# Embedding products between the row pairs, a last down group by token halves, residual joins divided

## The chip, the cores and the metric

One Trainium2 chip; the kernel runs on one core. The metric is the device time of one execution in microseconds. The profiled execution is one such run, recorded by the hardware profiler.

## What is computed

One layer of a hybrid decoder on 1024 tokens of width 1024, in float32. What matters here is its second half:

```
h = h + mixed @ w_o                                   # mixed: attention and convolution, normed
a = rms_norm(h, ln_ffn_g) @ w_up                      # 1024 -> 2 x 2816
gate, up = split(a); gate = causal_dwconv(gate) + b
h = h + (silu(gate) * up) @ w_down                    # 2816 -> 1024
h = h + sigmoid(rms_norm(h, ln_ple_g) @ w_pg) * (p @ w_pe)   # p: 256 wide
```

`p @ w_pe` (the embedding product) depends on the inputs alone. A norm's factor 1/rms belongs to a token, so a product's result can be multiplied by it afterwards.

## The kernel before

The engines: TensorE (PE) multiplies, VectorE (DVE), ScalarE (ACT) and GpSimd (POOL) do the rest, SyncE (SP) issues the transfers. Features lie on the 128 partitions, in 8 rows `m`; tokens lie along the free axis, in two halves `hf` of 512. Each float32 operand is split into a rounded high part and a remainder (`hi`, `lo`), and each product is three matmuls 128x512: hi x hi, hi x lo, lo x hi (`mm3`, L101 to L103). PSUM has 8 banks of 128x512, which the tiles take in turn; a matmul group into a bank waits until what lay there before has been read.

*Rows.* `mixed @ w_o` is made for half 1 first, 8 rows `bh`, and then for half 0 in four pairs of rows, `A0` to `A3`: rows k and k + 4, tiles `bp`, 24 matmuls a pair. What follows a row (`row_rest`, L887 to L904): VectorE multiplies by a factor and adds the residual (`hm`, also stored to memory as `hD`), ScalarE makes `y` = `hm` x gain and squares `hm`, into PSUM, and VectorE adds the squares up (`fssq`).

*Products by Strassen.* `@ w_up` is done as 7 products for each of 22 chunks of features, on 2x2 blocks of activations and weights (a Winograd form). The four differences t1 to t4 of a pair's blocks (`forms_of`, L906 to L922, GpSimd and VectorE) and their high and low parts (`keep_form`, L873, tiles `forms`) are made once. Products are called (f, i), chunk and number; each is 12 matmuls, into `ux`, `uy` or `uz`. Weight blocks and GpSimd's sums of them (`wsum`, L984) are split into `wbh` and `wbl` some products ahead. `uv` is ScalarE's copy of product 1 (L1058), which frees its PSUM tile for product 2.

The list `order` sets the sequence of pairs and products, and `behind(n, d, rank, fn)` puts what follows a product d places later. The instructions of each engine stand in the order of the program there; in the down groups a scheduler orders them.

*Down.* `@ w_down` sums over the 22 chunks in 6 groups (`GROUPS`: 3, 4, 4, 4, 4, 3 chunks). In each group and for each row m, weights are loaded and split (L140, L143), and both halves are multiplied (12 matmuls each for 4 chunks, 9 for 3) and added to `h` (L1154). `acth`, `actl` are the parts of a chunk's activations. In group 4 GpSimd multiplies `h` by the norm's factor `rfb` (L1160) and adds the residual `hD` (L1163). In group 5 VectorE multiplies the product by `rfb` (`t`, L1157) and adds it (L1158).

*End.* Then come 2 rows of embedding products `b`, the gated inputs `fh`, `fl` of all 8 rows over 1024 tokens (ScalarE L1198, VectorE L1199; squares L1206, summed on GpSimd L1207), and 8 rows of `@ w_pg`, with one further row of embedding products after each. The norm's factor is made behind the first half row: token sums on TensorE (L156), a VectorE step (L158), a power on GpSimd (L160), then spread over the partitions by small matmuls (L165). `finish_` is the rest of an output row.

## Time and profile before

| | us |
|---|---|
| median of 3 runs | 1489.42 (1489.16 to 1489.54) |
| profiled execution | 1490.71 |
| its span in the profile | 1488.9 |
| TensorE busy in the span | 1433.8 (96%) |
| VectorE, ScalarE, GpSimd busy | 990.5, 584.2, 492.6 |

The matmuls are pipelined: a record lasts about 0.4 us, but where nothing waits the next starts 0.23 us later. TensorE's idle time is therefore the measure, and its granted clock. In the page's 40 slices TensorE falls below nine tenths at the very start and in three later places; two concern us, the row pairs (632 to 720 us) and the end of the down groups (about 1325 to 1375 us).

### The profile page before, as it was taken

The page shows a single profiled execution, that of the slowest core. Times are in us where ns is not written, and L with a number is a line of the kernel's source. Part 1 is how long each engine was busy: PE and PEld are TensorE (multiplying, and loading weights), DVE is VectorE, ACT ScalarE, POOL GpSimd, SP SyncE. Part 2 cuts the span into 40 slices and gives each one's busy share as a digit, 9 for nine tenths or more (in the row PEclk, how much of TensorE's full clock was granted, in tenths as well). Part 3 has the DMA queues.
Part 4 walks back from the last instruction along what each step waited for, and adds up shares of the span by engine and source line. Part 5 has one row for each costly group of instructions (what it writes and reads, how often), then busy time and mean ns, then how long its engine had stood idle before and what let it go on. Part 6 is the DMA issues. An engine that isn't in the chain of part 4 may idle for free.

```text
span 1488.9 us, 19441 instructions
## 1 busy us (share of the span) xinstructions
PE 1433.8 (96%) x7207; PEld 1168.9 (79%) x7207; DVE 990.5 (67%) x1588; ACT 584.2 (39%) x1190; POOL 492.6 (33%) x467
## 2 busy tenths in 40 slices
PE   7999999998999999986999999999999999997998
PEld 6787898996777777765888888888888888876887
DVE  7645566546778888777777777877774344469533
ACT  4110131237868889653323333233335112125211
POOL 3221242465445558245223333333310000474000
PEclk9999999999989999997999999999999999999999
DMA  6221214300000002241222222222235123341211
GB/s 250 82 71 56 75 58 155 104 1 1 1 1 1 1 1 86 93 149 63 72 74 68 71 85 85 86 86 85 78 114 184 57 106 114 103 160 69 71 43 43
DMA packets 48190, 115.50 MB, mean 78 GB/s; under 512 B 5472, under 2 KB 8160, under 8 KB 48096
## 3 DMA queue, kind: packets, MB, share of 16 engines
q1 hardware_dynamic: 48096, 114.26, 22.8%
q8 instruction: 57, 0.93, 0.3%
q14 instruction: 37, 0.30, 0.1%
HBM read 90.12 MB, written 24.12 MB: 77 GB/s over the span
## 4 chain that ended last, share of the span: by engine, by line
PE 55%; DVE 6%; ACT 2%; issue 2%; DMA 1%; POOL 1%; SPq 0%; ACTq 0%; DVEq 0%; POOLq 0%
PE uy L1018 12%; PE uz L1018 8%; PE ux L1018 8%; PE ba L102 6%; PE ba L103 6%; PE ba L101 6%; PE bv L753 2%; PE ba L719 1%; DVE forms L881 1%; ACT P L683 1%; DVE h L1158 1%; PE b L666 1%; DVE t L1157 1%; PE b L101 1%; PE b L667 0%
## 5 line engine op out<-in xcount | busy, mean ns | idle before, releaser
L1018 PE MATMUL uy<-forms,wbh 128*128 128x512 f32 x528 | 166.6, 397 | 0.0
L694 POOL TENSOR_SCALAR P<-P,sc,consts 128x64 f32<-128x64 f32 (+8 forms) x192 | 129.2, 683 | 103.6 <-DVE sc L692 98.0
L984 POOL TENSOR_TENSOR wsum<-wup,wup 128x512 f32<-128x512 f32 x44 | 71.8, 1632 | 234.5 <-DMA wup<-in_w_up 201.6
L102 PE MATMUL ba<-actl,wh 128*128 128x512 f32 x352 | 138.1, 394 | 1.7 <-DVE actl L1140 1.6
L103 PE MATMUL ba<-acth,wl 128*128 128x512 f32 x352 | 137.5, 393 | 0.0
L101 PE MATMUL ba<-acth,wh 128*128 128x512 f32 x352 | 137.2, 393 | 0.0
L998 DVE TENSOR_TENSOR wbl<-wsum,wbh 128x512 fp32r<-128x512 f32 x88 | 79.8, 907 | 66.3 <-ACT wbh L997 66.3
L1018 PE MATMUL uz<-forms,wbh 128*128 128x512 f32 x352 | 112.8, 401 | 8.3 <-DVE forms L881 3.3
L1018 PE MATMUL ux<-forms,wbh 128*128 128x512 f32 x352 | 111.9, 399 | 9.2 <-ACT uv L1058 9.2
L677 DVE TENSOR_REDUCE nmax<-b 128x1 f32<-128x64 f32 (+8 forms) x192 | 96.7, 539 | 36.0 <-PE b L669 35.3
L1018 PEld LDWEIGHTS uy<-forms,wbh 128*128 128x128 f32 x528 | 100.3, 190 | 23.4
L683 ACT ACTIVATE P<-b,nmax 128x64 f32<-128x64 f32 (+8 forms) x192 | 108.9, 576 | 19.8 <-DVE sc L692 12.1
L143 DVE TENSOR_TENSOR wl<-wraw,wh 128x1024 fp32r<-128x1024 f32 (+3 forms) x93 | 92.2, 995 | 31.7 <-ACT wh L140 14.4
L1018 PE MATMUL uy<-forms,wbl 128*128 128x512 f32 x264 | 104.7, 396 | 0.0
L1154 DVE TENSOR_TENSOR h<-h,ba 128x512 f32<-128x512 f32 x64 | 43.8, 686 | 89.9 <-PE ba L103 89.8
L719 PE MATMUL ba<-consts,P 128*128 128x128 f32 x592 | 91.2, 278 | 5.3 <-DVE pl L735 2.5
L142 POOL TENSOR_SCALAR wh<-wraw 128x1024 fp32r<-128x1024 f32 (+2 forms) x37 | 47.9, 1298 | 133.3 <-PE b L102 46.1
L140 ACT CAST wh<-wraw 128x512 fp32r<-128x512 f32 (+2 forms) x56 | 35.3, 647 | 143.5 <-PE ba L102 119.6
L1160 POOL TENSOR_TENSOR h<-h,rfb 128x1024 f32<-128x1024 f32 x8 | 22.4, 2795 | 205.9 <-DVE h L1154 203.5
L719 PEld LDWEIGHTS ba<-consts,P 128*128 128x128 f32 x592 | 68.9, 143 | 23.9 <-issue 7.7
L1018 PEld LDWEIGHTS ux<-forms,wbh 128*128 128x128 f32 x352 | 67.1, 191 | 25.4 <-ACT uv L1058 9.6
L1018 PEld LDWEIGHTS uz<-forms,wbh 128*128 128x128 f32 x352 | 67.4, 192 | 24.8 <-DVE forms L881 3.6
(306 smaller groups left out, 3854.3 us busy)
## 6 DMA issues: line engine op xcount, KB each, us to landing
wup<-in_w_up SPq DMA_DIRECT2D x88, 256.0 KB, 4.1
aD<-ua SPq DMA_DIRECT2D x22, 512.0 KB, 2.9
t<-aD SPq DMA_DIRECT2D x22, 512.0 KB, 4.5
wraw<-in_w_down SPq DMA_DIRECT2D x32, 256.0 KB, 5.6
wraw<-in_wA SPq DMA_DIRECT2D x13, 512.0 KB, 3.6
hinc<-in_xT SPq DMA_DIRECT2D x16, 256.0 KB, 3.4
h<-t SPq DMA_DIRECT2D x16, 256.0 KB, 2.4
hin<-h SPq DMA_DIRECT2D x16, 256.0 KB, 4.2
```

The lines of the kernel that those rows point to most:

```text
L101: pe.matmul(ps, ah, bh, start=first, stop=False)
L102: pe.matmul(ps, ah, bl, start=False, stop=False)
L103: pe.matmul(ps, al, bh, start=False, stop=last)
L142: pool.tensor_scalar(hi, raw, 1.0, 1.0, op0=OP.mult, op1=OP.mult)
L143: dve.tensor_sub(lo, raw, f32(hi))
L677: dve.tensor_reduce(nmax[:, b:b + 1], ps[:, o:o + w], axis=AX.X, op=OP.max, negate=True)
L683: act.activation(pr[:, pc:pc + w], ps[:, o:o + w], AF.Exp, bias=nmax[:, b:b + 1], accum_out=den[:, b:b + 1])
L694: pool.tensor_scalar(pr[:, pc:pc + w], pr[:, pc:pc + w], sc[:, b:b + 1], gates[:, t, hd * 3 + b:hd * 3 + b + 1], op0=OP.mult, op1=OP.mult)
L719: pe.transpose(pt[0:k, r * P:(r + 1) * P], probs[u, r][:, pc:pc + k], ident)
L984: pool.tensor_tensor(t, a, b, op=op)
L998: dve.tensor_sub(lo, y, f32(hi))
L1018: pe.matmul(ps, a[:, k], b, start=new and k == n_mm == 0, stop=k == 3 and n_mm == 2, skip_group_check=not new)
```

## The change

1. The 96 matmuls of the embedding products go from the end to a place between the row pairs: the list now runs A0, E0, E1, E2, A1, E3, E4, E5, A2, E6, E7, (0,1), A3, (1,1), (0,2), (1,2). ScalarE copies each result to SBUF, it is stored to memory (`eD`) and loaded again in `finish_` (`ein`). Their weights and `p` are loaded and split beside the `bh` rows (from `mid` on).
2. What follows a pair is written anew (`pair_rest`, `pair_end`): all four differences on VectorE, squares to SBUF, the sums of squares last, and the parts of t2, t3, t4 beside the next pair.
3. The groups are 3, 4, 4, 4, 3, 4. The last takes all 8 rows for token half 0 and then all for half 1, with its weights kept in 8 buffers (`wd`), and the gated input of a row and half is made at once from the PSUM tile `bd`. The norm's sums and spread go by halves.
4. The residual joins: `irb` = 1/`rfb` is made before group 0 (8 spread matmuls); GpSimd multiplies `hD` by it and adds it to `h`, rows 0 to 3 in group 1 and rows 4 to 7 in group 2. All of `h` is then multiplied by `rfb` in the last group.

```
-GROUPS = (3, 4, 4, 4, 4, 3)
+GROUPS = (3, 4, 4, 4, 3, 4)
...
-        if m == 0:
-            act.square(fs, hm)
-        else:
-            act.square(ps, hm)
-            dve.tensor_add(fs, ps, fs)
...
+    def row_square(m, hf, hm):
+        sq = fssq[:, hf * 512:(hf + 1) * 512] if m == 0 else S([P, 512], F32, "t2", 4)
+        act.square(sq, hm)
+        return sq
+
+    def row_norm(m, hf, sq):
+        if m:
+            fs = fssq[:, hf * 512:(hf + 1) * 512]
+            dve.tensor_add(fs, fs, sq)
+
+    def sub(nm, k, a, b):
+        z = yf[nm, k] = S([P, 512], F32, f"yt1{k}" if nm == "t1" else "yt", 1 if nm == "t1" else 4)
+        dve.tensor_sub(z, a, b)
+
+    def form_hi(nm, k, y):
+        both = S([P, 2, 512], F32R, f"form{nm}{k}")
+        form[nm][k] = both[:, 0], both[:, 1]
+        act.copy(form[nm][k][0], y)
+
+    def form_lo(nm, k, y):
+        hi, lo = form[nm][k]
+        dve.tensor_sub(lo, y, f32(hi))
+
+    def pair_rest(k, tiles):
+
+        mm = (k, k + 4)
+        hms = [row_sum(m, 0, ps) for m, ps in zip(mm, tiles)]
+        pair_end(k - 1)
+        for m, hm in zip(mm, hms):
+            row_gain(m, 0, hm)
+        y11, y21, y12, y22 = (yf[m, hf] for hf in (1, 0) for m in mm)
+        form_hi("b22", k, y22)
+        sqs = [row_square(m, 0, hm) for m, hm in zip(mm, hms)]
+        sub("t1", k, y12, y11)
+        sub("t3", k, y22, y12)
+        form_hi("t1", k, yf["t1", k])
+        form_lo("b22", k, y22)
+        sub("t2", k, y22, yf["t1", k])
+        sub("t4", k, y21, yf["t2", k])
+        form_lo("t1", k, yf["t1", k])
+        for m, sq in zip(mm, sqs):
+            row_norm(m, 0, sq)
+
+    def pair_end(k):
+        if k >= 0:
+            for fn in (form_hi, form_lo):
+                for nm in ("t3", "t2", "t4"):
+                    fn(nm, k, yf[nm, k])
 
...
+        if m == 3:
+            mid = mark()
...
+    pT = [weights(d["pT"][k], 1024, tag="pT", bufs=2, after=mid, by_act=True) for k in range(2)]
+    wpe = [weights(d["w_pe"][i], 1024, tag="wpe", bufs=2, k=8, after=mid, by_act=True) for i in range(2)]
+    eD = [dram.tile([P, T], F32, name=f"eD_{m}") for m in range(KC)]
...
-    order = [("A", 0), ("A", 1), (0, 1), ("A", 2), (1, 1), ("A", 3), (0, 2), (1, 2),
+    order = [("A", 0), ("E", 0), ("E", 1), ("E", 2), ("A", 1), ("E", 3), ("E", 4), ("E", 5), ("A", 2), ("E", 6), ("E", 7),
+             (0, 1), ("A", 3), (1, 1), (0, 2), (1, 2),
              (0, 5), (0, 6), (0, 3), (0, 7), (1, 5), (0, 4), (1, 6), (1, 3), (1, 7)]
...
 
-    special = {("A", 1): lambda: norm_sums(1), (0, 1): lambda: norm_spread(1),
+    special = {("E", 1): lambda: norm_sums(1), ("E", 3): lambda: norm_spread(1),
                (0, 6): lambda: norm_sums(0), (0, 3): lambda: norm_spread(0)}
+
+    def embed(n, m):
+
+        wh, wl = (w[:, m % 4 * 2:m % 4 * 2 + 2] for w in wpe[m // 4])
+        for hf in range(2):
+            ps = PS("be", 2)
+            proj_fm(ps, wh, wl, *zip(*pT), hf)
+
+            def keep(hf=hf, ps=ps):
+                e = S([P, 512], F32, "emb", 2)
+                act.copy(e, ps)
+                nc.sync.dma_start(eD[m][:, hf * 512:(hf + 1) * 512], e)
+            behind(n, 0, 0, keep)
+
     def pair(n, k):
-        tiles = [PS("bp", 4) for _ in range(2)]
+        tiles = [PS("bp", 3) for _ in range(2)]
         for m, ps in zip((k, k + 4), tiles):
             row(m, 0, ps)
-        for m, ps in zip((k, k + 4), tiles):
-            behind(n, 0, 0, lambda m=m, ps=ps: row_rest(m, 0, ps))
-        behind(n, 0, 1, lambda: forms_of(k))
-        behind(n, 1, 1, lambda: forms_of(k, True))
+        behind(n, 0, 1, lambda: pair_rest(k, tiles))
+        if k == 3:
+            behind(n, 1, 1, lambda: pair_end(k))
...
-            if gi == len(GROUPS) - 2:
-                pool.tensor_mul(h[m], h[m], rfb)
-                r = S([P, T], F32, "t4", 4)
-                load(r, hD[m])
-                pool.tensor_add(h[m], h[m], r)
+    irb = S([P, T], F32, "irb")
+    with not_before(near):
+        for hf in range(2):
+            ir = S([P, 4], F32, "ir", 2)
+            dve.reciprocal(ir, norm[hf])
+            spread_all(ir, 4, irb[:, hf * 512:(hf + 1) * 512])
+
+    def down(gi, m, w, acts, hf):
+        s = slice(hf * 512, (hf + 1) * 512)
+        ps = psa() if gi < len(GROUPS) - 1 else PS("bd", 5)
+        proj_fm(ps, *w, [a[0] for a in acts], [a[1] for a in acts], hf)
+        if gi == 0:
+            act.copy(h[m][:, s], ps)
+        elif gi < len(GROUPS) - 1:
+            dve.tensor_add(h[m][:, s], h[m][:, s], ps)
+        else:
+            dve.tensor_add(ps, ps, h[m][:, s])
+            dve.tensor_mul(ps, ps, rfb[:, s])
+            gated_input(m, hf, ps)
+
+
+    pssq = S([P, T], F32, "pssq")
+    eh, el = ([[], []] for _ in "hl")
+
+    def gated_input(k, hf, ps):
+
+        s = slice(hf * 512, (hf + 1) * 512)
+        g = small["g_ple"][:, k:k + 1]
+        hi = S([P, 512], F32R, f"fh{hf}{k}")
+        lo = S([P, 512], F32R, f"fl{hf}{k}")
+        act.activation(hi, ps, AF.Copy, scale=g)
+        dve.scalar_tensor_tensor(lo, ps, g, f32(hi), op0=OP.mult, op1=OP.subtract)
+        eh[hf].append(hi)
+        el[hf].append(lo)
+        if k == 0:
+            act.square(pssq[:, s], ps)
+        else:
+            sq = S([P, 512], F32, "t2", 4)
+            act.square(sq, ps)
+            (pool if k < KC - 1 else dve).tensor_add(pssq[:, s], pssq[:, s], sq)
+        act.copy(h[k][:, s], ps)
...
+        here = mark()
+        w = {}
+        for mm, hfs in ([((m,), (0, 1)) for m in range(KC)] if gi < len(GROUPS) - 1 else
+                        [(range(KC), (0,)), (range(KC), (1,))]):
+            for hf in hfs:
+                for m in mm:
+                    if hf == 0:
+                        w[m] = weights(d[f"w_down{gi}"][m], n * P, *(("w", 4) if gi < len(GROUPS) - 1 else ("wd", KC)), k=n,
+                                       after=near if gi == 0 else None, by_act=True)
+                    down(gi, m, w[m], acts, hf)
+            m = mm[0]
+            if gi in (1, 2) and m // 4 == gi - 1:
+                r = S([P, T], F32, "hres", 2)
+                load(r, hD[m], here)
+                pool.tensor_mul(r, r, irb)
+                pool.tensor_add(h[m], h[m], r)
...
+            proj_fm(ps, wh, wl, eh[c // 512], el[c // 512], c % 512 // w, w)
             done.append((m, s, w, ps))
-            if m == c == 0:
+            if m == 0:
                 with not_before(mark()):
-                    rp = rstd(pssq, NT, D, "rp")
-            if m == 0 and c:
-                with not_before(mark()):
-                    spread_all(rp, NT, rpb, psb)
+                    rp = rstd(pssq[:, s], 4, D, "rp", 2)
+                    spread_all(rp, 4, rpb[:, s], psb)
```

*ScalarE, up to a `uv` copy that a product 2 waits for.* Before, up to the copy of product (0,1); `forms` are high parts of a pair's differences, `y` the rows with gain.

```order
L880 CAST forms_1536_7177<-yt_7182 128x512
L880 CAST forms_1536_7177<-yt_7180 128x512
L880 CAST forms_1536_7177<-yt_7245 128x512
L880 CAST forms_1554_7255<-y_0_1551_7241 128x512
L880 CAST forms_1554_7255<-yt_1553_7253 128x512
L1087 COPY rfb_7081<-ba_7278 128x512
L880 CAST forms_1554_7255<-yt_7260 128x512
L880 CAST forms_1554_7255<-yt_7258 128x512
L880 CAST forms_1554_7255<-yt_7286 128x512
L997 CAST wbh_7294<-wup_7116 128x512
L1058 COPY uv_7277<-ux_7264 128x512
```

Now, from the rows of the fourth pair to the copy of product (1,1); `formt` and `formb` are the high parts, `t` a square.

```order
L890 ACTIVATE y_0_1658_7628<-hm_7614,consts_61 128x512
L909 CAST formb_1659_7630<-y_0_1658_7628 128x512
L894 ACTIVATE t_1660_7632<-hm_7610 128x512
L894 ACTIVATE t_1661_7634<-hm_7614 128x512
L909 CAST formt_1664_7640<-yt_1662_7636 128x512
L1023 CAST wbh_7650<-wsum_7544 128x512
L909 CAST formt_1672_7670<-yt_7638 128x512
L909 CAST formt_1673_7672<-yt_7643 128x512
L909 CAST formt_1674_7674<-yt_7645 128x512
L1023 CAST wbh_7679<-wsum_7574 128x512
L1084 COPY uv_7667<-ux_7654 128x512
```

Before, the high parts of two pairs stood ahead of the first copy; now one pair's rest and the third pair's last three parts stand ahead of the second copy (the first stands earlier).

*VectorE in the last down group.* Before, products of rows 5 and 6 (`h_2284`, `h_2285`) and low parts of rows 2 and 3; `t` is the product times `rfb`, `fl` the low part.

```order
L1157 TENSOR_TENSOR t_2602_12435<-ba_12425,rfb_7081 128x512
L1157 TENSOR_TENSOR t_2607_12454<-ba_12444,rfb_7081 128x512
L1158 TENSOR_TENSOR h_2284_10767<-h_2284_10767,t_2602_12435 128x512
L1158 TENSOR_TENSOR h_2285_10768<-h_2285_10768,t_2607_12454 128x512
L1199 SCALAR_TENSOR_TENSOR fl_2638_12566<-h_2281_10764,consts_61,fh_2637_12565 128x1024
L1157 TENSOR_TENSOR t_2609_12467<-ba_12457,rfb_7081 128x512
L1199 SCALAR_TENSOR_TENSOR fl_2641_12573<-h_2282_10765,consts_61,fh_2640_12572 128x1024
L1158 TENSOR_TENSOR h_2285_10768<-h_2285_10768,t_2609_12467 128x512
```

Now, the first rows of the last group; `bd` is the product in PSUM.

```order
L1200 TENSOR_TENSOR bd_12448<-bd_12448,h_2357_10988 128x512
L1201 TENSOR_TENSOR bd_12448<-bd_12448,rfb_7124 128x512
L1200 TENSOR_TENSOR bd_12475<-bd_12475,h_2358_10989 128x512
L1201 TENSOR_TENSOR bd_12475<-bd_12475,rfb_7124 128x512
L1215 SCALAR_TENSOR_TENSOR fl_2650_12464<-bd_12448,consts_61,fh_2649_12463 128x512
L1200 TENSOR_TENSOR bd_12504<-bd_12504,h_2359_10990 128x512
L1215 SCALAR_TENSOR_TENSOR fl_2656_12491<-bd_12475,consts_61,fh_2655_12490 128x512
L1201 TENSOR_TENSOR bd_12504<-bd_12504,rfb_7124 128x512
```

The add into `h` and the low part over 1024 tokens have become an add, a product and a low part over 512, each with `bd` as an input.

*TensorE at the norm of the end.* Before, behind the first half row of `@ w_pg`, the sums of all 8 token blocks; the spread stands 24 matmuls later.

```order
L102 MATMUL ba_12608<-fl_2653_12601,wh_12548 128x512
L103 MATMUL ba_12608<-fh_2652_12600,wl_12549 128x512
L156 MATMUL ba_12633<-consts_61,pssq_12552 128x1 x8
L101 MATMUL ba_12646<-fh_2632_12553,wh_12548 128x512
L102 MATMUL ba_12646<-fl_2633_12554,wh_12548 128x512
L103 MATMUL ba_12646<-fh_2632_12553,wl_12549 128x512
```

Now, behind the same half row, the sums of one half.

```order
L102 MATMUL ba_12861<-fl_2698_12665,wh_12857 128x512
L103 MATMUL ba_12861<-fh_2697_12664,wl_12858 128x512
L156 MATMUL ba_12886<-consts_61,pssq_11013 128x1 x4
L101 MATMUL ba_12901<-fh_2701_12687,wh_12857 128x512
L102 MATMUL ba_12901<-fl_2702_12688,wh_12857 128x512
L165 MATMUL bb_12895<-consts_61,rpr_12893 128x128 x4
L103 MATMUL ba_12901<-fh_2701_12687,wl_12858 128x512
```

The spread `bb` has moved up to two matmuls behind the sums, and the same stands once more behind the second half row.

## Rows read from the trace of the kernel before

**Rows 1.** The page, part 1: busy us, share of the span, instructions.

```profile
PE 1433.8 (96%) x7207; PEld 1168.9 (79%) x7207; DVE 990.5 (67%) x1588; ACT 584.2 (39%) x1190; POOL 492.6 (33%) x467
```

**Rows 2.** Windows: us, then per engine busy us (instructions); clock, DMA share, GB/s.

```profile
632.00:720.00 88.00, 70.45 (x289) 56.16 (x288) 66.34 (x86) 38.75 (x67) 40.73 (x29) 0.86 0.27 90
...
720.00:1112.50 392.50, 392.50 (x1690) 318.05 (x1689) 302.68 (x364) 131.09 (x203) 126.23 (x73) 1.00 0.25 84
```

**Rows 3.** TensorE's waits, whole span: us in total, times, longest.

```profile
PE ux L1018 <- ACT uv L1058: 9.2, 1, 9.2
...
PE ba L102 <- DVE actl L1140: 1.6, 1, 1.6
```

**Rows 4.** TensorE's timeline behind the row pairs: start, us, what, [idle before].

```profile
674.05 1.22 PE L1018 MATMUL ux<-forms,wbh 128*128 128x512 f32 x2 [9.20 <-ACT uv L1058]
...
678.06 0.65 PE L1018 MATMUL ux<-forms,wbh 128*128 128x512 f32 x2
...
683.96 0.50 PE L1018 MATMUL uz<-forms,wbh 128*128 128x512 f32 x1 [2.94 <-ACT forms L880]
687.73 0.80 PE L1018 MATMUL uz<-forms,wbh 128*128 128x512 f32 x1 [3.26 <-DVE forms L881]
...
691.98 0.39 PE L1018 MATMUL uy<-forms,wbl 128*128 128x512 f32 x1
...
695.98 1.19 PE L1018 MATMUL uz<-forms,wbh 128*128 128x512 f32 x2 [2.14 <-DVE uw L1026]
...
701.24 1.42 PE L165 MATMUL ba<-consts,rfr 128*128 128x128 f32 x8
```

**Rows 5.** VectorE's timeline, pieces from three stretches of the span.

```profile
676.90 0.68 DVE L894 TENSOR_TENSOR bp<-bp,rab 128x512 f32<-128x512 f32 x1
...
1324.96 2.76 DVE L1140 TENSOR_TENSOR actl<-t,acth 128x1024 fp32r<-128x1024 f32 x1
...
1341.64 0.68 DVE L1157 TENSOR_TENSOR t<-ba,rfb 128x512 f32<-128x512 f32 x1
1342.25 2.16 DVE L143 TENSOR_TENSOR wl<-wraw,wh 128x384 fp32r<-128x384 f32 x1
...
1345.53 1.21 DVE L143 TENSOR_TENSOR pTl<-wraw,pTh 128x1024 fp32r<-128x1024 f32 x1
```

**Rows 6.** VectorE by line, 632 to 700 us: busy, mean ns | idle before.

```profile
L896 DVE TENSOR_TENSOR hm<-bp,hin 128x512 f32<-128x512 f32 x8 | 5.5, 691 | 0.3
...
L904 DVE TENSOR_TENSOR fssq<-bp,fssq 128x512 f32<-128x512 f32 x7 | 4.8, 692 | 9.1 <-ACT bp L903 9.1
```

**Rows 7.** TensorE's timeline at the first embedding products.

```profile
1361.27 0.47 PE L101 MATMUL b<-pTh,wpeh 128*128 128x512 f32 x1 [2.35 <-DVE t L1157]
...
1363.88 0.40 PE L103 MATMUL b<-pTh,wpel 128*128 128x512 f32 x1
1369.80 0.80 PE L101 MATMUL b<-pTh,wpeh 128*128 128x512 f32 x1 [5.53 <-DVE t L1157]
...
1374.78 0.40 PE L101 MATMUL ba<-fh,wh 128*128 128x512 f32 x1
```

**Rows 8.** ScalarE by line, 632 to 700 us.

```profile
L899 ACT ACTIVATE y<-hm,consts 128x512 f32<-128x512 f32 x10 | 7.2, 723 | 20.1 <-DVE hm L896 20.1
L903 ACT ACTIVATE bp<-hm 128x512 f32<-128x512 f32 x7 | 4.1, 582 | 0.0
...
L1058 ACT COPY uv<-ux 128x512 f32<-128x512 f32 x2 | 1.2, 576 | 0.0
```

**Rows 9.** A spread at the start (timeline), and the norm's power by line.

```profile
40.18 1.95 PE L165 MATMUL ba<-consts 128*128 128x128 f32 x16
...
L160 POOL TENSOR_TENSOR rfr<-rfv,consts 128x4 f32<-128x4 f32 x2 | 2.0, 1020 | 9.0 <-DVE rfv L158 9.0
```

**Rows 10.** GpSimd's timeline in the down groups.

```profile
1323.38 3.25 POOL L1163 TENSOR_TENSOR h<-h,t 128x1024 f32<-128x1024 f32 x1
...
1341.40 2.58 POOL L1207 TENSOR_TENSOR pssq<-pssq,t 128x1024 f32<-128x1024 f32 x1 [8.75 <-ACT t L1206]
```

More of the change, by code (lines that the diff above doesn't have):

```diff
@@ L865, in load_h0 @@
         load(hins[m, hf], h0[m][:, hf * 512:(hf + 1) * 512], after)
-    FORMS = ("b11", "b21", "t1", "b22", "t2", "t3", "t4")
-    form = {nm: [None] * 4 for nm in FORMS}
-    yf, forms_ = {}, {}
+    form = {nm: [None] * 4 for nm in ("b11", "b21", "t1", "b22", "t2", "t3", "t4")}
+    yf = {}
     hD = [dram.tile([P, T], F32, name=f"hD_{m}") for m in range(KC)]
-    def keep_form(nm, k, y):
-        i = FORMS.index(nm)
-        where = i < 2, k
-        if where not in forms_:
-            forms_[where] = S([P, 2 if i < 2 else 5, 2, 512], F32R, f"forms{i < 2:d}{k}")
-        hi, lo = (forms_[where][:, i if i < 2 else i - 2, z] for z in range(2))
-        act.copy(hi, y)
-        dve.tensor_sub(lo, y, f32(hi))
-        form[nm][k] = hi, lo
     def row(m, hf, ps):
@@ L898, in row_rest @@
         y = yf[m, hf] = S([P, 512], F32, f"y{m}_{hf}")
[L899 to L924 removed]
+        act.activation(y, hm, AF.Copy, scale=small["g_ffn"][:, m:m + 1])
@@ L991, in split @@
     def split(n):
-        if n < len(order) and order[n][0] != "A":
+        if n < len(order) and order[n][0] not in ("A", "E"):
             f, i = order[n]
@@ L1002, in ahead @@
         for j in (n + AHEAD + 5, n + AHEAD + 2):
-            if j < len(order) and order[j][0] != "A":
+            if j < len(order) and order[j][0] not in ("A", "E"):
                 f, i = order[j]
@@ L1111, in _emit @@
                     pair(n, i)
+                elif w == "E":
+                    embed(n, i)
                 else:
@@ L1141, in act_parts @@
         return hi, lo
-    def down_group(gi, acts):
-        n = GROUPS[gi]
-        for m in range(KC):
-            wh, wl = weights(d[f"w_down{gi}"][m], n * P, k=n, after=near if gi == 0 else None, by_act=True)
-            for hf in range(2):
-                s = slice(hf * 512, (hf + 1) * 512)
-                ps = psa()
-                proj_fm(ps, wh, wl, [a[0] for a in acts], [a[1] for a in acts], hf)
-                if gi == 0:
-                    act.copy(h[m][:, s], ps)
-                elif gi < len(GROUPS) - 1:
-                    dve.tensor_add(h[m][:, s], h[m][:, s], ps)
-                else:
-                    t = S([P, 512], F32, "t2", 4)
-                    dve.tensor_mul(t, ps, rfb[:, s])
-                    dve.tensor_add(h[m][:, s], h[m][:, s], t)
-            if gi == len(GROUPS) - 2:
-                pool.tensor_mul(h[m], h[m], rfb)
-                r = S([P, T], F32, "t4", 4)
-                load(r, hD[m])
-                pool.tensor_add(h[m], h[m], r)
+    irb = S([P, T], F32, "irb")
@@ L1211, in finish_ @@
     def finish_(m, s, w, ps):
+        e = S([P, 512], F32, "ein", 2)[:, 0:w]
+        load(e, eD[m][:, s], here)
         t = S([P, 512], F32, "t2", 4)[:, 0:w]
@@ L1214, in finish_ @@
         act.activation(t, t, AF.Sigmoid)
-        dve.tensor_mul(t, emb[m][:, s], t)
+        dve.tensor_mul(t, e, t)
         o = S([P, 512], F32, "o", 2)[:, 0:w]
@@ L1220, in _emit @@
     for m in range(KC):
-        wh, wl = wpg.pop() if wpg else weights(d["w_pg"][m], 1024, k=KC, by_act=True)
+        wh, wl = weights(d["w_pg"][m], 1024, k=KC, by_act=True)
         for c, w in ((0, 512), (512, 512)) if m < KC - 1 else ((0, 512), (512, 256), (768, 256)):
```

74 lines of the change are left out of this document (13 added, 61 removed).

## The prediction

> **What bounds the kernel now.** I read the page's busy shares first, then the table of stretches, then TensorE's waits, then its timeline around each long wait, and last the queues that those waits name. TensorE is busy 1433.8 us of the span [rows 1], so time can only come from its gaps, its low clock, or work taken from it. Between 720 and 1112.5 us it never stops: 392.50 us for 1690 matmuls [rows 2], which is 0.2322 us for one. That is the price of a matmul below. Between 632 and 720 us it is busy only 70.45 of 88 us at a granted clock of 0.86 [rows 2]; this is the stretch of the four row pairs and of the first products. The longest wait of all is here, 9.2 us for a ScalarE copy; another, of 1.6 us, stands in the down groups, for a low part of the activations [rows 3].
>
> What the stretch of the pairs loses now, from the timeline [rows 4]: idle 9.20 + 2.94 + 3.26 + 2.14 = 17.5 us. Behind three of these waits the matmuls start 0.43 us apart, which is the 1.2 GHz level: 9 of them from 674.05 to 678.06 (4.01 where 2.09 would do), 10 from 687.73 to 691.98 (4.25 for 2.32), 12 from 695.98 to 701.24 (5.26 for 2.79). That is 6.3 us more, 23.9 in all. The cause is VectorE's queue. TensorE had left all pair rows before its wait began at 664.85, yet VectorE came to the last pair only at 676.90 [rows 5]: it stood still 9.1 us for squares that ScalarE writes to PSUM [rows 6], its subtractions were stretched by GpSimd, and so the copy behind them in ScalarE's queue was late.
>
> What the end loses: 1.58 us (the 1.6 of [rows 3]), 2.35 and 5.53 idle, and behind the last 12 matmuls in 4.98 us instead of 2.79 [rows 7]: 2.2. Together 11.7 us.
>
> **The change part by part.** *Embedding products.* 8 x 12 matmuls, 96 x 0.2322 = 22.3 us, leave the end and stand between the pairs: nothing gained on TensorE, but now 36 matmuls (8.4 us) lie behind each of the first two pairs and 36 behind the third (two embedding rows and product (0,1)). A pair thus gives VectorE 24 + 36 matmuls, 13.9 us. Its work for a pair is now 15 operations (four on the new rows, four differences, five low parts, two sums), at 0.61 to 0.69 us [rows 5, 6] 9.2 to 10.4 us. So the queue no longer falls behind; the squares go to SBUF and their sums stand last, so the 9.1 us wait goes too. Sixteen ScalarE copies at 0.58 us [rows 8], 9.3 us, fall beside ScalarE work that fills 38.75 of the 88 us [rows 2].
>
> What is late next: (a) The first embedding product needs the split of the loaded weights. Four more low parts of 1024 columns (1.21 us each [rows 5]) stand in VectorE's queue beside the last rows; two or three lie ahead of the product, which begins 5.6 us after the pair's start. I count 5.1 to 6.4 us of queue behind the pair's start, so a wait of 0.5 us, bounds 0 and 5. (b) The copy that freed PSUM for product (1,2). From the end of the fourth pair's rows TensorE has (1,1) and (0,2), 24 matmuls, 5.6 us. VectorE needs two operations for the last row (1.4), three low parts of the third pair, then five operations to the difference t4, 8 x 0.65 = 5.2: t4 is there after 6.6 us. ScalarE then rounds t4, rounds a weight block, and copies: 3 x 0.6 = 1.8 us. The copy is done 8.4 us after the rows, so the wait is 2.9 us instead of 9.2; bounds 0 (ScalarE reaches it with the queue empty) and 9.2. Whether the clock falls in it is open: it did not behind 2.35 us [rows 7], it did behind 2.14 and 3.26 [rows 4]. I take half of the 1.9 to 2.5 us, 1.0. (c) The wait for a subtraction before (0,3), 2.14 now, I put at 0.95, since the small reciprocal step still stands ahead of it. Left: 0.5 + 3.9 + 0.95 = 5.35; gain 23.9 - 5.35 = **18.5 us**, bounds 7 and 24.
>
> On the clock, the Trainium skill ("TensorE: Matmul & The Clock Gate", Part 1) holds that an idle array falls back to 1.2 GHz. [...]
>
> *Last down group by halves.* Its 16 tiles cost TensorE 12 matmuls each, 2.79 us. For a tile VectorE has an add, a product and a low part, all with PSUM as an input: 3 x 0.61 to 0.69, at most 2.1 us; ScalarE rounds with gain, squares and copies, 0.72 + 0.58 + 0.58 = 1.9 us [rows 8]. Both keep up, and when the last tile of half 1 is done the first output product has half 0 ready and long enough work on it (24 matmuls, 5.6 us) to cover that tile's own chain. The 2.35 and 5.53 us waits and the 2.2 us of low clock have no place any more. What it adds: the norm's sums now come per half, and the spread stands two matmuls (0.46 us) behind the sums, where before 24 stood between. The chain is a VectorE step of 0.15 us, a GpSimd power of 1.02 us [rows 9] and two handovers, 1.4 us: 0.9 us of wait, twice, bounds 0 and 2.5 each (a busy VectorE queue). The output products after that are as before, and the tail behind the last matmul does not change.
>
> *Residual joins.* 16 GpSimd passes move from the last but one group to groups 1 and 2. They need 1/norm spread over the tokens: 8 more small products on TensorE, whose 16 records took 1.95 us at the kernel's start [rows 9]; I take 1.8, bounds 1.0 and 3.5 (two ScalarE copies wait behind). What they hold up: a low part of only 384 columns took 2.16 us beside a GpSimd pass, while a product of 512 columns from PSUM in the same pass took 0.68 [rows 5, 10]. The 1.58 us wait of now is such a case: the low part of an activation took 2.76 us while GpSimd was joining [rows 5, 10]. That meeting now falls on the end of group 2 instead; I leave 1.6 us there, bounds 0 and 3.2.
>
> The Trainium skill ("SBUF — State Buffer", "Who interferes with whom") states it as a rule: a VectorE instruction with two SBUF inputs contends with a GpSimd instruction that reads SBUF, and the one that starts later is blocked for the whole of the other. By that rule 8 GpSimd passes per group can hold VectorE for up to 22 us of a group's 44.6; its own work there is 16 adds, 8 splits and 4 low parts of 1024, about 21 us at the durations of [rows 5]. The two together still fit, so by the rule the sum stays as it is, and only the boundary pays, as the row shows.
>
> Sum of this end: 11.7 - (1.6 + 0.9 + 0.9 + 1.8) = **6.5 us**. Stores and reloads of the embedding products are 16 of 256 KB each way in stretches where the DMA engines are a quarter busy (0.27 and 0.25 [rows 2]); I count nothing, and they are not needed until hundreds of us later.
>
> Total 18.5 + 6.5 = 25.0 us. The profiled execution took 1490.71 us (span 1488.9); 1465.7 for it, and with the median of the runs 1.3 us lower, 1464.5 us.
>
> **The rivals.** *The copy is as late as now.* If GpSimd's sums of weight blocks hold the pair's subtractions (2.16 us instead of at most 0.69, so 1.5 us each [rows 5, 10]), four of them behind the third and fourth pair bring the wait back to about 9.2 us with its 1.9 us of low clock: 7.2 us worse than my 3.9, 1472. For it: the same blocks are still prepared by GpSimd ahead of the first products. Against it: GpSimd has lost its 12 differences there.
>
> *The waits are a chain, not a queue.* Then the embedding products only push everything later and the stretch keeps its 23.9 us; only the end is won: 1490.71 - 6.5 - 1.3 = 1483. Against it: 676.90 against 664.85 is a queue that is behind.
>
> *Nothing waits.* All of 0.5, 3.9, 0.95, 1.8 and 1.6 us vanish: 1456.
>
> *Slower: the last group becomes bound by VectorE.* Place: the 16 tiles of the last group, where GpSimd adds a square in each. Point from which it decides: the gain of 25.0 us spread over 16 tiles is 1.56 us, so from 2.79 + 1.56 = 4.35 us for a tile on the kernel is slower. If two of a tile's three operations were held by a 512 GpSimd pass of about 1.3 us (half of the 2.58 us of [rows 10]), a tile would take 2.0 + 2.6 = 4.6 us: 29 us lost, 1493. For it: holding is seen in [rows 5]. Against it: only for operations without a PSUM input, and of these the tiles have one in 16.
>
> **How the numbers follow.** Forecast (1461 to 1468) 0.55; the late copy 0.20; nothing waits 0.10; the chain 0.07; the parts cancel and it is within 0.2% 0.03; slower 0.05. 0.2%, 3 us, is what a measurement can tell from no change. Faster 0.92, same 0.03, slower 0.05. The range reaches to the late copy with a small wait more, 1477, and half way to no wait at all, 1457; left out are the chain, no change, slower, and half of the lowest case, 0.20.
>
> **What would show it.** In the profile after, the stretch of the pairs (from 632 us, 22.3 us of products longer) should have TensorE busy all but about 5 us, one wait of 2 to 4 us for the copy of product (1,1) and VectorE's first operation of the fourth pair within 1 us of that pair's first row. At the end no wait for the down group's product; two waits near 1 us at the norm's spread; one near 1.6 us between groups 2 and 3. Wrong would be: a wait over 6 us behind the fourth pair, tiles of the last group more than 2.9 us apart, or embedding products waiting for ScalarE's copies.

## The result, and the profile after

The changed kernel took 1470.67 us (median of four runs, 1464.96 to 1474.31) against 1489.48 us before: a ratio of 0.9867, 95% interval 0.9832 to 0.9902, so 18.8 us faster. The forecast of 1464.5 us was 6 us too fast and within its range. The profiled run is the fastest of the four, 1464.96 us with a span of 1463.1, and that is within 1 us of the 1465.7 us worked out for it. This agreement is partly luck. In the profile before, TensorE began the first row pair at 632.03 us; in this one at 626.07, and the change did not make that difference: the embedding weights' loads and splits now stand beside the `bh` rows ahead of that point, yet TensorE takes 29.56 us from its first `bh` matmul to the first pair row, and took 29.55 before. What the change did is read from the first pair row to the end: 856.9 us before, 837.0 after, 19.9 us less where I had 25.0. By the median alone, the rival of the copy as late as before (1472) is nearer than the forecast; it is the waits below that tell the two apart.

The stretch from the first pair row to the down groups, and the rest: us, TensorE's busy us (its records), granted clock, DMA share, GB/s. Before:

```profile
632.03:1112.57 480.54, 462.99 (x1978) 0.98 0.25 85
1112.57:1488.90 376.33, 362.26 (x1593) 0.99 0.28 96
```

After:

```profile
626.07:1113.26 487.19, 479.98 (x2073) 1.00 0.28 95
1113.26:1463.10 349.84, 340.76 (x1513) 0.99 0.32 109
```

With the 22.3 us of embedding products put on the same side, the first stretch won 15.6 us (480.5 to 464.9) and the second 4.2 (354.0 to 349.8). I had 18.5 and 6.5.

TensorE's waits from 600 us on, in the changed kernel, which answer to [rows 3] (total us, times, longest; `be` is an embedding product, `bb` the spread of the norm at the end, `rpr` its power):

```profile
PE ux L1044 <- ACT uv L1084: 5.1, 1, 5.1
PE bb L165 <- POOL rpr L160: 2.5, 2, 1.7
PE ba L102 <- DVE actl L1181: 1.9, 1, 1.9
PE uz L1044 <- DVE uw L1052: 0.9, 1, 0.9
PE be L103 <- DVE wpel L143: 0.4, 1, 0.4
PE uy L1044 <- ACT wbh L1023: 0.3, 1, 0.3
PE uy L1044 <- DVE uc L1052: 0.2, 1, 0.2
```

Every wait that was forecast is there, and only two small ones (0.3 and 0.2) that were not. The largest is still the ScalarE copy, at 5.1 us where 2 to 4 was to show. TensorE's timeline there and at the norm's spread, which answers to [rows 4, 7]:

```profile
680.94 0.40 PE L1044 MATMUL ux<-formb,wbl 128*128 128x512 f32 x1
686.45 1.22 PE L1044 MATMUL ux<-formb,wbh 128*128 128x512 f32 x2 [5.11 <-ACT uv L1084]
687.47 0.63 PE L1044 MATMUL ux<-formb,wbl 128*128 128x512 f32 x1
```

```profile
1378.15 1.34 PE L165 MATMUL bb<-consts,rpr 128*128 128x128 f32 x8 [1.69 <-POOL rpr L160]
1379.14 0.78 PE L103 MATMUL ba<-fh,wl 128*128 128x512 f32 x1
...
1382.57 0.39 PE L102 MATMUL ba<-fl,wh 128*128 128x512 f32 x1
```

Behind the copy 6 matmuls start 0.43 us apart, behind the second spread 7: 1.3 and 1.5 us of low clock. There are no waits at the first output product, where 2.35 and 5.53 us stood [rows 7].

Why the copy was late, from VectorE's timeline behind the fourth pair (the first line is its last row operation):

```profile
676.90 0.69 DVE L884 TENSOR_TENSOR hm<-bp,hin 128x512 f32<-128x512 f32 x1
677.50 2.99 DVE L913 TENSOR_TENSOR formt<-yt,formt 128x512 fp32r<-128x512 f32 x3
680.41 2.36 DVE L904 TENSOR_TENSOR yt<-y,y 128x512 f32<-128x512 f32 x2
```

and GpSimd's at the same time:

```profile
678.02 1.32 POOL L1010 TENSOR_TENSOR wsum<-wup,wup 128x512 f32<-128x512 f32 x1 [10.65 <-DMA wup<-in_w_up]
680.62 1.60 POOL L1010 TENSOR_TENSOR wsum<-wsum,wup 128x512 f32<-128x512 f32 x1 [1.28 <-DVE formt L913]
```

VectorE had almost no backlog left. TensorE ended the fourth pair's last row at 675.77 us and VectorE's first operation on it began at 676.17; before the change that lag was 18.1 us. For the first row of the pair the lag was 1.9 us (672.96 to 674.84), where I had said within 1. Then three low parts lasted 2.99 us and two differences 2.36, each group beside a GpSimd sum of weight blocks: one of the three took 1.79 us and one of the two 1.76, the others 0.68.

### The profile page after: what moved, and what is told of

Its sections match the earlier page's. It is cut to its first block, busy times and chain, and to the rows that moved or that the text cites. A ratio compares the mean times of both kernels' runs of the same rounds, so it can differ in the third digit from the quotient of the medians.

```text
span 1463.1 us, 19683 instructions
## 1 busy us (share of the span) xinstructions
PE 1423.8 (97%) x7223; PEld 1161.9 (79%) x7223; DVE 990.0 (68%) x1612; ACT 605.1 (41%) x1240; POOL 477.5 (33%) x462
## 4 chain that ended last, share of the span: by engine, by line
PE 50%; DVE 2%; issue 1%; ACT 0%; POOLq 0%; POOL 0%; ACTq 0%; DVEq 0%
PE uy L1044 12%; PE uz L1044 8%; PE ux L1044 8%; PE ba L103 6%; PE ba L102 6%; PE ba L101 6%; PE bd L103 1%; PE bd L102 1%; PE bd L101 1%; DVE wbl L1024 0%; DVE actl L1181 0%; DVE yt L904 0%; PE ba L165 0%; POOLq L1365 0%; DVE ua L1071 0%
## 5 line engine op out<-in xcount | busy, mean ns | idle before, releaser
L1044 PE MATMUL uy<-formt,wbh 128*128 128x512 f32 x528 | 165.2, 394 | 0.7 <-ACT wbh L1023 0.3
L1044 PEld LDWEIGHTS uy<-formt,wbh 128*128 128x128 f32 x528 | 99.0, 188 | 24.9 <-issue 1.2
L1044 PE MATMUL ux<-formb,wbh 128*128 128x512 f32 x352 | 111.6, 398 | 5.1 <-ACT uv L1084 5.1
L102 PE MATMUL ba<-actl,wh 128*128 128x512 f32 x288 | 113.3, 394 | 1.9 <-DVE actl L1181 1.9
L103 PE MATMUL ba<-acth,wl 128*128 128x512 f32 x288 | 112.9, 393 | 0.0
L101 PE MATMUL ba<-acth,wh 128*128 128x512 f32 x288 | 112.1, 392 | 0.0
L1044 PE MATMUL uy<-formt,wbl 128*128 128x512 f32 x264 | 104.4, 395 | 0.0
L1071 DVE SCALAR_TENSOR_TENSOR ua<-ug,consts,ua 128x1023 f32<-128x1023 f32 (+1 forms) x44 | 85.1, 1933 | 0.0
L735 DVE TENSOR_TENSOR pl<-ba,ph 128x512 fp32r<-128x512 f32 x120 | 78.8, 679 | 7.5 <-ACT ph L731 6.3
L1044 PEld LDWEIGHTS ux<-formb,wbh 128*128 128x128 f32 x352 | 67.0, 191 | 21.1 <-ACT uv L1084 5.5
```

The costliest lines, as they stand in the source:

```text
L101: pe.matmul(ps, ah, bh, start=first, stop=False)
L102: pe.matmul(ps, ah, bl, start=False, stop=False)
L103: pe.matmul(ps, al, bh, start=False, stop=last)
L735: dve.tensor_sub(pl, pt[0:k], f32(ph))
L1044: pe.matmul(ps, a[:, k], b, start=new and k == n_mm == 0, stop=k == 3 and n_mm == 2, skip_group_check=not new)
L1071: dve.scalar_tensor_tensor(a[:, j:], y[:, 0:T - j], cw[:, 2 - j:3 - j], a[:, j:], op0=OP.mult, op1=OP.add)
```

## Experiments

All are edits of the changed kernel; "from the first pair row" is the time from there to the end of the profiled span, 837.0 us in the changed kernel.

**The changed kernel again.** 

> The changed kernel once more, unchanged. Its four runs lay between 1464.96 and 1474.31 us, and the profiled one, the fastest, came to the first row pair 5.96 us earlier than the profiled run before, in code that the change does not touch. Theory 1: the 9 us between runs come from the stage before 626 us, where stretches at 1.2 GHz come and go; then this profile has its span above or below 1463.1 us by as much as the first pair row starts after or before 626.07 us, and from that row to the end it takes 837.0 us within 1 us. Theory 2: the spread arises in the changed places, for instance a longer stretch at 1.2 GHz behind the 5.1 us wait or behind the norm's spread; then the time from the first pair row to the end moves with the span, by up to 9 us.

Measured: 1471.53 us (1468.17 to 1473.72), ratio 0.9869 (0.9847 to 0.989). The first pair row started at 628.83 us and 837.5 us remained: theory 1. The clock in the stage ahead, which the change leaves alone, shows where the difference comes from. Stretches of it in the kernel before (us, TensorE's busy us, clock, DMA share, GB/s):

```profile
48.00:72.00 24.00, 21.89 (x99) 0.93 0.26 81
344.00:368.00 24.00, 20.70 (x128) 1.00 0.00 1
400.00:432.00 32.00, 29.39 (x169) 0.84 0.00 1
```

The same stretches in the changed kernel's first profile:

```profile
48.00:72.00 24.00, 21.89 (x106) 1.00 0.21 67
344.00:368.00 24.00, 21.97 (x133) 0.93 0.00 1
400.00:432.00 32.00, 29.38 (x199) 1.00 0.00 1
```

Three places in the attention stage run at 1.2 GHz in some executions and not in others (a fourth, at about 208 us, in the profiles of two later runs). In the profile before, the one between 400 and 432 us alone cost 5 us (0.84 of 32 us is 10 us at half rate), which is most of the 6.0 us between the two first profiles. Over all profiles of this study the first pair row starts between 626.07 and 635.97 us. So single runs differ by 5 to 10 us from there, and I compare profiles from the first pair row on.

**Embedding products last.** The products stand behind the last up product; their weights are loaded and split shortly before.

```
-    order = [("A", 0), ("E", 0), ("E", 1), ("E", 2), ("A", 1), ("E", 3), ... ("E", 7), (0, 1), ("A", 3), (1, 1), (0, 2), (1, 2),
...
+    order = [("A", 0), ("A", 1), (0, 1), ("A", 2), (1, 1), ("A", 3), (0, 2), (1, 2),
...
+    order += [("E", m) for m in range(KC)]
...
```

> The embedding products stand behind the last up product instead of between the pairs; the new work behind a pair is kept. Theory: the place is what lets VectorE keep up. Its 15 operations of 9.2 to 10.4 us for a pair then meet 24 to 36 matmuls (5.6 to 8.4 us), it falls 2 to 4 us behind per pair, and the copy behind the fourth pair comes late: the wait before product (1,2) or (0,2) grows from 5.1 to 9 to 13 us, with a stretch at 1.2 GHz behind it; 5 to 10 us slower than the changed kernel from the first pair row to the end. Rival: the new order of the operations and the squares kept out of PSUM do it alone; then the waits behind the pairs stay within 2 us of the changed kernel's 6 us.

Measured: 1488.81 us (1484.83 to 1494.04), ratio to before 0.9993 (0.9975 to 1.001): nothing is left of the gain. From the first pair row 854.2 us remained, 17.2 more than in the changed kernel. Its waits behind the pairs (632 to 720 us):

```profile
PE ux L1042 <- DVE wbl L1022: 3.2, 1, 3.2
PE uz L1042 <- DVE uw L1050: 2.2, 1, 2.2
PE ux L1042 <- ACT rfb L1111: 1.6, 1, 1.6
PE uz L1042 <- DVE formt L913: 1.2, 1, 1.2
PE ba L165 <- POOL rfr L160: 1.2, 1, 1.2
PE uy L1042 <- DVE wbl L1022: 0.7, 1, 0.7
```

These are 10.1 us and 4.3 of low clock behind them, 14.4 against 8.1 in the changed kernel: 6 us, within the 5 to 10 of the theory, though spread over VectorE's queue and not at the one copy. VectorE came to the fourth pair's last row 8.6 us after TensorE had ended it. The other 11 us are not the missing cover. About 9 us were lost where the products and their splits now stand: waits of 2.6, 2.1 and 1.5 us at the last up products and 2.9 us of low clock. The rest, 1.7 us, is low clock behind the unchanged wait at the end of group 2, which came in this execution and not in the changed kernel's two.

The run shows something else. Behind the pairs the sequence of pairs and products is that of the kernel before, where 23.9 us were lost; the new work behind a pair alone saves 9.5 of them.

**The work behind a pair as before.** Squares into PSUM, three differences on GpSimd, embedding products kept between the pairs.

```
...
-        behind(n, 0, 1, lambda: pair_rest(k, tiles))
...
+            behind(n, 0, 0, lambda m=m, ps=ps: old_rest(m, ps))
+        behind(n, 0, 1, lambda: old_forms(k))
+        behind(n, 1, 1, lambda: old_forms(k, True))
```

> The embedding products stay between the pairs, but what follows a pair is done as before the change: squares into PSUM with the sums right behind, three of four differences on GpSimd. Before the change VectorE took 14.85 us from the third pair's first operation (662.05) to the fourth's (676.90) with this work; the pairs now give it 13.9 us. Theory: both parts are needed, VectorE falls about 1 us behind per pair, and the fourth pair's differences wait for GpSimd: the wait at the copy is 7 to 10 us instead of 5, 3 to 6 us slower than the changed kernel's 837.2 us from the first pair row to the end. Rival: the place of the products alone does it; within 1.5 us.

Measured: 1471.11 us (1467.49 to 1472.61), 836.5 us from the first pair row. The wait at the copy is longer, as the theory said:

```profile
PE ux L1077 <- ACT uv L1117: 7.8, 1, 7.8
```

but the total is the changed kernel's. Behind the pairs 10.5 us are lost (8.9 idle, 1.6 of low clock) against 8.1, and VectorE's lag at the fourth pair's last row is 4.6 us. The changed kernel loses these 2.4 us again later: 0.7 in small waits and 1.4 that I can't place before the down groups, 0.7 behind the last spread. The low clock behind the second spread came in this run too, at about 1.5 us, partly in the spread's own small matmuls.

The rival holds for the total. Together with the run before it gives four cases, by the loss behind the pairs and VectorE's lag at their last row: old work and no products between them 23.9 and 18.1 us; new work alone 14.4 and 8.6; products alone 10.5 and 4.6; both 8.1 and 0.4. Either part takes more than half of the backlog away; with the products in place the new work is worth only 2.4 us.

**GpSimd's sums left out for two chunks.**

```
+            if f < 2:
+                return fetch(f, a)
```

> Leaves out GpSimd's sums of weight blocks for chunks 0 and 1 (the first block stands in for the sum), so that GpSimd is idle beside the last two pairs; all else as in the changed kernel. Theory: the wait at the copy was 4.8 to 5.1 us and not the 2.9 us forecast because these passes stretch VectorE's subtractions behind the fourth pair (three low parts 2.99 us instead of 1.87, two differences 2.36 instead of 1.28); then the wait comes out at 2.4 to 3.4 us. Rival: the rest of the chain was counted too short; it stays above 4.3 us.

Measured, in one profiled execution: a wait of 2.64 us at the copy, and VectorE's same pieces are

```profile
677.50 1.88 DVE L913 TENSOR_TENSOR formt<-yt,formt 128x512 fp32r<-128x512 f32 x3
679.31 1.28 DVE L904 TENSOR_TENSOR yt<-y,y 128x512 f32<-128x512 f32 x2
```

1.88 for 2.99 and 1.28 for 2.36: 2.2 us, the difference between 5.1 and the 2.9 forecast. VectorE also waited 0.89 and 1.39 us for TensorE at the two rows of the pair, so the lag of the changed kernel is gone too. The holding by GpSimd is the cause.

Other runs bear it out with the sums kept. In three of them (the two with gated inputs late, and the changed kernel with the group sizes of before) the sums fell beside the third pair's low parts, of which three took 4.1 to 5.0 us; the fourth pair's pieces then took 1.89 and 1.29, VectorE's lag at its last row was 1.0 to 1.9 us, and the wait at the copy came to 3.6 to 4.5. Which pieces are held differs from execution to execution, and the wait with it.

**Copies ahead of the fourth pair.**

```
-    order = [..., ("A", 1), ("E", 3), ("E", 4), ("E", 5), ("A", 2), ("E", 6), ("E", 7), (0, 1), ("A", 3), (1, 1), (0, 2), (1, 2),
+    order = [..., ("A", 1), ("E", 3), ("E", 4), ("E", 5), ("E", 6), ("A", 2), ("E", 7), (0, 1), (1, 1), ("A", 3), (0, 2), (1, 2),
```

> Product (1,1) is moved ahead of the fourth pair, so that its copy stands before that pair's work in ScalarE's queue; one embedding row moves ahead of the third pair to make room. Theory: the 5.1 us wait is the place of the copy in the queue alone; it goes, and what is late next is the low part of the fourth pair's difference t1 for product (0,5): a wait of 0 to 2.5 us. From the first pair row to the end 4 to 6 us less than 837.0. Rival: the fourth pair's work itself is the limit, and the whole 5 us wait comes back before (0,5) or (0,6): within 1.5 us of the changed kernel.

Measured: 1466.52 us (1462.42 to 1468.23), ratio 0.9833 (0.981 to 0.9856). From the first pair row to the down groups 482.5 us instead of 487.2: 4.7 less. The 5 us wait is gone and what is late next is small (0.7 and 2.2 us). To the end it is 834.6 us, only 2.4 less: the unchanged wait of 1.89 us at the end of group 2 had 1.7 us of low clock behind it in this run, and one of 0.74 us stood ahead of it.

**The last group row by row.**

```
-        for mm, hfs in ([((m,), (0, 1)) for m in range(KC)] if gi < len(GROUPS) - 1 else
-                        [(range(KC), (0,)), (range(KC), (1,))]):
+        for mm, hfs in ([((m,), (0, 1)) for m in range(KC)]):
```

> The last group runs row by row, both halves of a row, as the other groups do; the gated inputs are still made per row and half from PSUM. Theory: what removed the 2.35 and 5.53 us waits is that the gated input is made at once and in PSUM, with 24 matmuls of cover behind it, and not the order of the halves: the time from the first row of the last group to the end stays within 1.5 us. Rival: the halves are needed, since the last row's tiles come directly before the output products; then waits of 2 us or more appear at the first output product's last terms.

Measured: 1469.97 us (1468.74 to 1473.59); 350.7 us from the down groups to the end instead of 349.8, with no new wait; 1.6 us of low clock behind the wait at the end of group 2 came in this run. The halves are worth nothing here.

**Gated inputs late.** As the last, and the gated inputs made 1024 wide from finished rows.

```
-            dve.tensor_mul(ps, ps, rfb[:, s])
-            gated_input(m, hf, ps)
+            dve.tensor_mul(h[m][:, s], ps, rfb[:, s])
...
+    for m in range(KC):
+        gated_input(m)
```

> The embedding products stay between the pairs, but the gated inputs are made as before the change, from the finished rows, 1024 tokens at a time, and the last group runs row by row. Theory: before the change 24 embedding matmuls stood behind the last down row and still the waits were 2.35 and 5.53 us; without them the whole chain of VectorE and of GpSimd's 1024 wide sums is open: waits of 6 to 12 us at or in the first output product, with 2 us of low clock behind; from the first row of the last group to the end 8 to 13 us more than the changed kernel's 146.6 us. Rival: the old waits were made by the embedding weights' splits in VectorE's queue, which are gone from there; then at most 4 us more.

Measured: 1471.4 us (1468.02 to 1478.34). Between 1300 and 1400 us TensorE has no wait but the spread's:

```profile
PE bb L165 <- POOL rpr L160: 2.5, 2, 1.7
```

From the down groups to the end it took 352.1 us, with 1.6 us of low clock at the end of group 2. My theory fell: no wait of 6 to 12 us, none at all.

**The same, and the group sizes of before** (`GROUPS` = 3, 4, 4, 4, 4, 3). 

> As gates_late (last group row by row, gated inputs 1024 wide from finished rows), and the group sizes as before the change, so that the last group has 3 chunks. gates_late with 4 chunks had no wait at the output products at all. Theory formed from it: the length of the last group decides. A row gives VectorE 5.6 us of matmuls with 4 chunks and 4.2 with 3, and its work on a row is about 4.9 us (four operations of 0.69 at 0.61 to 0.73 from start to start, a low part of 1.28, a share of the last splits): with 3 chunks it falls behind 0.7 to 1.5 us a row, 6 to 12 in all, of which the first half row of the output product covers 5.6: waits of 2 to 7 us before or in the first output products. Rival: the embedding weights' splits and the joins beside the last group made the old waits; then no wait above 1 us here either.

Measured: 1472.8 us (1471.03 to 1474.03), one wait of 0.2 us at the sums besides the spread's, 352.0 us from the down groups to the end. The theory formed from the run before fell too; the rival's "no wait above 1 us" is what came.

**The changed kernel with the group sizes of before.** 

> The changed kernel, by halves and with gated inputs per tile from PSUM, with the group sizes as before the change: the last group has 3 chunks. Theory: a tile then gives 2.09 us of matmuls to three VectorE operations of 2.0 us, so it just keeps up; waits of 0 to 1.5 us in the last group or at the output products, and within 2 us of the changed kernel from the first group to the end (349.8). If both this and gates_late are free of waits and gates_late_three is not, either edit alone was enough. Rival: the tiles fall behind and 3 us or more are waited for.

Measured: 1473.07 us (1466.54 to 1478.33), 350.1 us from the down groups to the end, no new wait.

**All residual joins in group 3.**

```
-            if gi in (1, 2) and m // 4 == gi - 1:
+            if gi == 3:
```

> The residual joins of all 8 rows in group 3 instead of four rows each in groups 1 and 2. Theory: 16 GpSimd passes of about 2.8 us fill the 44.6 us of the group, so the last of them meet the low parts of the next group's activations, and the 1.9 us wait at the end of group 2 goes and one of 2 to 5 us comes at the end of group 3; 0 to 4 us slower. Rival: dividing the joins is worth nothing; the wait of about 1.9 us only moves by one group.

Measured: 1470.15 us (1464.63 to 1471.41), 836.9 us from the first pair row. The 1.9 us wait at the end of group 2 is gone, and none came at the end of group 3: 347.0 us from the down groups to the end, 2.8 less. Neither theory nor rival said so, and why the joins meet nothing there stays open. The total does not show it, since this run lost 1.5 us more at low clock behind the copy and 1.4 in small waits. Dividing the joins over two groups gains nothing over one group; it made the 1.9 us wait.

**The spread later.** Spread of a half 24 matmuls behind its sums.

```
-            if m == 0:
+            if m == 0 or (m, c) == (1, 0):
...
+                    if rps:
+                        o = c ^ 512
+                        spread_all(rps[o], 4, rpb[:, o:o + 512], psb)
...
```

> The spread of each half's norm stands 24 matmuls behind its sums instead of two. Theory: the two waits of 0.77 and 1.69 us are the VectorE step and the GpSimd power with too little cover; both go, and the 0.9 to 1.5 us of low clock behind the second with them: 3.4 to 4 us less from the first row of the last group to the end (146.6 us in two profiles of the changed kernel). Rival: the wait is one for VectorE's or GpSimd's queue and moves along: within 1 us.

Measured: 1464.68 us (1461.25 to 1469.39), ratio 0.9835 (0.9812 to 0.9859). Both waits and their low clock are gone: from the down groups to the end 345.2 us instead of 349.8, 4.6 less, where 3.4 to 4 was expected.

**Three edits together.** Copies first, spread later, and the joins of group 2 ahead:

```
-            if gi in (1, 2) and m // 4 == gi - 1:
+            if gi in (1, 2) and m < 4:
+                j = m + 4 * (gi - 1)
...
```

> Three edits together: the copies ahead of the fourth pair (as in the run before), the spread 24 matmuls behind its sums, and the joins of group 2 made for rows 4 to 7 while rows 0 to 3 run, so that GpSimd is done before the group ends. Theory: each works in its own place: about 3 to 5 us at the pairs, 3.4 to 4 at the spread, 1.5 to 3.5 at the end of group 2 (a wait of 1.9 us, in some profiles with 1.7 to 2.1 us of low clock behind it): 827 to 830 us from the first pair row to the end, against 837.2, and below both kernels. Rival: the joins' meeting with VectorE only shifts within the group and the wait stays: 831 to 833.

Measured: 1456.08 us (1453.77 to 1459.69), ratio to before 0.9776 (0.9757 to 0.9795): faster than both kernels. 825.1 us from the first pair row, 11.9 less than the changed kernel. Two of the edits gave 4.7 and 4.6 us in their own stretches; the third, which was not run alone, took away the wait of 1.9. Its waits from 620 us to the end, no matmul at low clock behind any:

```profile
PE uz L1044 <- DVE uw L1052: 2.2, 1, 2.2
PE be L103 <- DVE wpel L143: 1.0, 1, 1.0
PE uy L1044 <- DVE wbl L1024: 0.7, 1, 0.7
PE uy L1044 <- ACT wbh L1023: 0.4, 1, 0.4
```

## Why the prediction was right, and where it was not

**The losses before.** 17.5 us idle and 6.3 at low clock behind the pairs, 11.7 at the end: 35.6. In the changed kernel the same count gives 0.4 (embedding weights), 5.1 and 1.3 (copy, its low clock), 0.9 and 0.5 (small waits), 2.0 (the records of the spread of 1/norm), 1.9, 2.5 and 1.5 (activation part, norm's spread, its low clock): 16.1. The difference, 19.5, is the 19.9 measured. So the method held, and the gap to 25.0 lies in what I left for after: 10.6 instead of 16.1.

**(b) The copy, 2.9 us forecast, 5.1 measured.** This term was mis-sized by GpSimd's holding, which I priced only in the first rival. The run without the sums gives 2.64 us. The late copy was rival and forecast in one: the mechanism of the rival at a third of its size, two subtractions held 1.1 us each where it had four of 1.5. The Trainium skill ("SBUF — State Buffer", "Who interferes with whom") has the rule, that VectorE instructions with two SBUF inputs contend with GpSimd instructions that read SBUF; the trace agrees, with 2.99 against 1.88 us for the same three low parts.

**The clock.** I took 1.0 us behind the copy; 1.3 came (1.3 to 2.9 in all profiles with this wait). Behind the spread I took none and 1.5 came. That is a missing term.

**The spread, 1.8 us forecast, 2.5 measured.** The first of its two waits was 0.77 us, as reckoned; the second was 1.69, because the power took 1.93 us there and 1.01 for the first half. Beside it VectorE was splitting a weight block:

```profile
1376.00 1.23 DVE L143 TENSOR_TENSOR wl<-wraw,wh 128x1024 fp32r<-128x1024 f32 x1
1376.16 1.93 POOL L160 TENSOR_TENSOR rpr<-rpv,consts 128x4 f32<-128x4 f32 x1 [7.39 <-DVE rpv L158]
```

In the run with the spread later the same split fell beside the first power, and there the first took 1.94 us and the second 1.01; with the three edits together it fell beside neither, and both took 1.01. So GpSimd is held by VectorE as well as the other way round, which my sum left out. (c), (a) and the activation part (0.95, 0.5, 1.6 forecast; 0.94, 0.40, 1.88 measured) were sized well.

**The embedding products as cover.** Right, but not the whole. Without them between the pairs the loss there is 14.4 us and not 8.1, and all of the gain is gone; more than half of what is lost, however, was lost at the place to which that run moved them. I gave the gain at the pairs to both parts together; the new work alone saves 9.5 us of it and the products alone 13.4. "The waits are a chain" is refuted by the changed profile, in which VectorE's lag fell from 18.1 us to 0.4.

**The last group.** The gain came, and my reason for it was wrong. I put it down to the gated input by tiles and to the 24 matmuls of cover. Neither the halves, nor the tiles, nor the group's length brings a wait back in the four runs that undo them. What is left are parts that no run put back. Three take work or holding out of VectorE's queue: the embedding weights' splits, gone from there; the new form of the join, by which a product's add and its multiplication both read PSUM; and GpSimd's residual joins, which stood in the group ahead. (The last group's own weight buffers and PSUM tiles were not put back either.) VectorE by line from 1325 to 1376 us speaks for the second. Before (busy, mean ns | idle before):

```profile
L1158 DVE TENSOR_TENSOR h<-h,t 128x512 f32<-128x512 f32 x16 | 15.5, 977 | 0.3
L1199 DVE SCALAR_TENSOR_TENSOR fl<-h,consts,fh 128x1024 fp32r<-128x1024 f32 x6 | 11.9, 1993 | 0.0
...
L143 DVE TENSOR_TENSOR wl<-wraw,wh 128x384 fp32r<-128x384 f32 (+1 forms) x6 | 9.4, 1574 | 0.0
```

With gated inputs late and 3 chunks, where the same GpSimd passes of 1024 run:

```profile
L1200 DVE TENSOR_TENSOR bd<-bd,h 128x512 f32<-128x512 f32 x16 | 11.1, 695 | 1.8 <-PE bd L103 1.8
L1201 DVE TENSOR_TENSOR h<-bd,rfb 128x512 f32<-128x512 f32 x16 | 11.1, 691 | 0.5
L1213 DVE SCALAR_TENSOR_TENSOR fl<-h,consts,fh 128x1024 fp32r<-128x1024 f32 x8 | 10.2, 1278 | 1.3 <-ACT fh L1212 1.3
```

Before, adds took 977 ns and low parts 1993, held beside GpSimd; here the adds take 695 and the low parts 1278, and VectorE waits for TensorE instead of the other way. The low parts have two SBUF inputs in both, so the form of the join is not all of it. The timeline before speaks for the third part: the joins ran on into the last group, until 1332.66 us (GpSimd's rows and VectorE's, in order of time).

```profile
1326.59 3.39 POOL L1160 TENSOR_TENSOR h<-h,rfb 128x1024 f32<-128x1024 f32 x1
1327.64 2.75 DVE L143 TENSOR_TENSOR wl<-wraw,wh 128x384 fp32r<-128x384 f32 x1
1330.06 2.60 POOL L1163 TENSOR_TENSOR h<-h,t 128x1024 f32<-128x1024 f32 x1
...
1331.10 2.10 DVE L1158 TENSOR_TENSOR h<-h,t 128x512 f32<-128x512 f32 x1
...
1333.72 0.54 DVE L143 TENSOR_TENSOR wl<-wraw,wh 128x384 fp32r<-128x384 f32 x1
1334.19 0.68 DVE L1158 TENSOR_TENSOR h<-h,t 128x512 f32<-128x512 f32 x1
```

A weight split and an add took 2.75 and 2.10 us beside them, and 0.54 and 0.68 right after: 3.6 us. Three embedding splits in this stretch were 3.6 us more (1.21 each, two for `p` and one for the weights). How the old 7.9 us divide among the three stays open.

**The slower rival** had its place in the last group: its tiles never made TensorE wait, even at 2.09 us for a tile.

## What to carry to other kernels

Count what a queue has to do in a stretch against what the bounding engine gives it there, and put independent products where that count is negative: here 96 matmuls cost TensorE the same everywhere, and between the pairs they were worth 6.3 us with the new work and 13.4 with the old. Price one held subtraction of two SBUF operands for each GpSimd pass beside them, here 1.8 us instead of 0.68 for 512 columns, also where GpSimd has lost some of its work. A chain through two engines behind a small product (sums, power, spread) wants cover: two matmuls left 2.5 us of waits here, 24 left none.
